# A layer norm and an RMS norm whose factors go through a DRAM row: one change to a hybrid encoder kernel

## The chip, the cores and the metric

The kernel runs on one NeuronCore of a Trainium2 chip. The metric is device time in microseconds (us) for one execution. Engines are named as the profile names them: PE multiplies matrices (PEld loads its weights), DVE is the vector engine, ACT the scalar engine, POOL the GpSimd engine, SP the engine that issues most DMAs. POOL can issue DMAs of its own; it writes their pieces in software.

## The reference, cut to what matters

The reference is one layer of an encoder on an input of 1024 positions by 1024 channels, in float32. Two of its norms are touched:

```
def _rmsnorm(x, w):
    y = x * rsqrt(mean(x * x, axis=-1) + EPS)
    return y * w

def _layernorm(x, w, b):
    mu = mean(x, axis=-1)
    var = mean(square(x - mu), axis=-1)
    return (x - mu) * rsqrt(var + EPS) * w + b

a = silu(_layernorm(_dwconv_centred(glu(...)), ln_w, ln_b))     # 512 channels
...
x  = x + y @ w_out
h2 = _rmsnorm(x, ffn_norm_w)                                    # 1024 channels
x  = x + (silu(dwconv3(h2 @ W_gate)) * (h2 @ W_up)) @ W_down
```

The kernel keeps channels on the 128 partitions and positions along the free axis, so both norms sum over partitions, and the factor of each position has to be spread to all 128 partitions again.

## The kernel before, in words

Every big product is made with float32 values split in two parts of a rounded type (`split`: ACT copies the high part, DVE subtracts it to get the low part), three matmuls of 128x128 weights by 128x512 columns for each pair (`mm3`, lines 148 to 150). Most products run as `pair_job`s: two column blocks of weights are multiplied with one set of activations by seven products instead of eight, in the order 1, 2, 6, 7, 5, 4, 3. Each product is 12 matmuls here. Products 1, 6, 5 and 3 share one PSUM bank (`mm`), 7 and 4 share another (`sc`), 2 has its own (`tr`). When a bank takes its next product, the earlier contents must have been copied out: by ACT at line 440 (tile `su`) for products 1, 6 and 7, so product 6 cannot start before the copy of product 1 is done, product 5 not before the copy of product 6, product 4 not before the copy of product 7.

The norms are slotted between the pieces of such streams. `s_pairs.fill(n)` lets the stream of in-projection pairs advance by n pieces of six matmuls; the statements of the norm stand between two fills. PE keeps exactly the order in which the program states its work; on the other engines a scheduler places instructions when it is built, and then each engine runs its list strictly in order. So an instruction that waits holds back all that stand behind it on its engine.

The layer norm (loop at line 1056, one pass for each half of the positions): the channel sum of the four tiles (`total`) is multiplied by a matrix of ones in plain float32 (line 1065), which gives the mean on all partitions; DVE subtracts it (L1067); ACT squares (L1071); four small matmuls against a column of ones (L611) leave the variance of position 128c+p in column c of a 128x4 tile `r`; DVE copies it out (L615), POOL multiplies and raises to the power -0.5 (L592, L593). To spread it, `spread` makes four diagonal matrices (ACT, L600), multiplies them by ones in plain float32 (L601) and copies the result from PSUM (ACT, L602). Then DVE scales the four tiles (L1077, L1078), ACT applies silu (L1079) and the result is split (tile `ch`) and stored.

The FFN norm does the same for both halves, called `early`: there POOL makes the diagonals (L621). The scaling is late: `evac` of the first FFN job multiplies by `rstd2` (L1682, L1683), and the low parts of the activations of products 4 and 3 of that job (tile `hy`) are made by DVE at the same time. The names `hy`, `wq` and `wp` are the split activations and the split weights of that stream.

`x2_evac`, which ends each out-projection, stores the gained result `g` of all 16 tiles into the DRAM scratch `d_h2`. Later code reads back four of them: those of the second half of positions with index 4 to 7.

Of the kernel before, what the change touches and what calls it, by code (L numbers as in the profile page):

```python
# [18 lines left out]
P = 128  # L19
# [28 lines left out]
def tile_hybrid_encoder(  # L48
# [51 lines left out]
    def bank(tag):  # L100
        return ps.tile([P, H], F32, tag=tag, name=nm(tag), bufs=BANKS[tag])
# [4 lines left out]
    def tmp():  # L106
        return page(mp, "tm", 4)
# [375 lines left out]
    G.memset(mhalf, -0.5)  # L483
    ones_m = cp.tile([P, P], F32, name="ones_m")
    cp.tile([P, ALIGN // 4 - 8], F32, name="offset")
# [83 lines left out]
    d_x2 = scratch("d_x2", ND, 2)  # L569
    d_h2 = scratch("d_h2", ND, 2)  # L570
    d_t4 = scratch("d_t4", ND // 2)
# [22 lines left out]

    def spread(r, b, rs, diag=None, late=False):

        if diag is None:
            diag = tmp()
            for c in range(4):
                A.activation(diag[:, c * P : (c + 1) * P], ident, AF.Copy, scale=r[:, c : c + 1])  # L600
        T.matmul(b, ones_m, diag, start=True, stop=True)  # L601
        do = A.copy(rs, b)  # L602
        if late:
            pin(do)
        return rs

    def rstd_over_partitions(sq, n, tag, rs, early=False):
# [8 lines left out]
        rstd_small(r, r, n, early)  # L616
        diag = None
        if early:
            diag = tmp()
# [436 lines left out]
    for half in range(2):  # L1056
# [7 lines left out]
        mean = bank("ob")  # L1064
        T.matmul(mean, ones_m, total(xs, tmp()), start=True, stop=True)
        for t in xs:
# [6 lines left out]
        next(rstd)  # L1073
        s_pairs.fill(5)
        rs = next(rstd)
# [505 lines left out]
    def x2_evac(i):  # L1581


        def evac(half, acc):
# [178 lines left out]
    for k in range(NK2):  # L1763
        late_parts(5 + k // 2, 3, fetch(d_h2[k + NK2][1]))
    s_ffn.fill(7)
# [303 lines left out]
```

## Time and profile before

| quantity | value |
|---|---|
| median of three runs | 1721.42 us (1721.3 to 1722.16) |
| span of the profiled execution, first to last instruction | 1720.0 us |
| between the span and the median of the runs | 1.4 us |
| PE busy | 1699.1 us, 99% of the span |
| DVE busy | 1256.6 us, 73% |
| ACT busy | 825.0 us, 48% |
| POOL busy | 240.7 us, 14% |
| mean granted PE clock | 0.998 |

The layer norm runs at 406 to 476 us of the span, the out-projection at about 970 to 1055 us and the FFN norm at 1059 to 1078 us. In the rows of the timeline the columns are: start in us, length in us, engine, line, operation, output and input tiles, shapes, how many instructions are merged, and in brackets the idle time ahead with what ended it. Matmul rows overlap, since matmuls are pipelined: the distance between two starts is the time that one costs.

### The profile page before, as it was taken

The numbers are of one execution on the slowest core, as the hardware profiler recorded it, in microseconds if no ns is written. First come the engines' busy times: TensorE is split into PE (matmuls) and PEld (weight loads), VectorE is DVE, ScalarE is ACT, GpSimd is POOL, SyncE is SP. The second block draws the span as 40 slices with busy tenths as digits, with TensorE's granted clock in tenths as the row PEclk, the third lists the DMA queues.
The fourth block names the chain that finished last, engine by engine and source line by source line (L and its number), as shares of the span: only waits on it lengthen the run. The fifth ranks groups of instructions, "written<-read, shape, count | busy, mean of one in ns | idle before, by whom it ended". The sixth has DMA issues, their size and how long they took to land.

```text
span 1720.0 us, 30762 instructions
## 1 busy us (share of the span) xinstructions
PE 1699.1 (99%) x11902; PEld 1416.2 (82%) x11902; DVE 1256.6 (73%) x1937; ACT 825.0 (48%) x1544; POOL 240.7 (14%) x281
## 2 busy tenths in 40 slices
PE   8999999999999999999999999999999999999998
PEld 6878888788788888888888888888888888888787
DVE  4599999745779888888656466667777776657865
ACT  6443443233577777776442245444434433542334
POOL 1212222200001111111100002122222222000110
PEclk9999999999999999999999999999999999999999
DMA  8777888854673444435689466577778776783842
GB/s 281 238 181 177 201 191 189 203 160 148 202 261 91 146 127 133 128 116 200 223 277 279 143 205 199 147 159 153 165 166 174 171 172 154 229 266 102 215 95 99
DMA packets 337096, 308.28 MB, mean 179 GB/s; under 512 B 17582, under 2 KB 249142, under 8 KB 336950
## 3 DMA queue, kind: packets, MB, share of 16 engines
q1 hardware_dynamic: 289590, 267.51, 49.1%
q0 software_dynamic: 47360, 38.81, 15.5%
q8 instruction: 93, 1.52, 0.4%
q14 instruction: 53, 0.43, 0.1%
HBM read 201.40 MB, written 87.03 MB: 168 GB/s over the span
## 4 chain that ended last, share of the span: by engine, by line
PE 61%; DVE 1%; ACT 1%; DMA 0%; issue 0%; POOLq 0%; ACTq 0%; SPq 0%; DVEq 0%
PE mm L148 14%; PE mm L150 14%; PE mm L149 14%; PE sc L148 3%; PE sc L150 3%; PE sc L149 3%; PE ob L1375 2%; PE tr L148 1%; PE tr L150 1%; PE tr L149 1%; PE sc L1197 1%; PE sc L1283 1%; PE mm L1334 1%; PE sc L1334 1%; PE ob L1197 0%
## 5 line engine op out<-in xcount | busy, mean ns | idle before, releaser
L148 PE MATMUL mm<-hx,wp 128*128 128x512 f32 x1068 | 426.9, 400 | 2.3 <-ACT tm L851 1.4
L150 PE MATMUL mm<-hx,wp 128*128 128x512 f32 x1068 | 416.9, 390 | 0.5 <-DVE wp L124 0.5
L149 PE MATMUL mm<-hx,wp 128*128 128x512 f32 x1068 | 416.2, 390 | 0.0
L124 ACT CAST wp<-wr 128x1024 fp32r<-128x1024 f32 (+2 forms) x147 | 147.3, 1003 | 217.8 <-PE mm L149 180.3
L148 PEld LDWEIGHTS mm<-hx,wp 128*128 128x128 f32 x1068 | 200.6, 188 | 45.0 <-DVE ev L800 2.2
L150 PEld LDWEIGHTS mm<-hx,wp 128*128 128x128 f32 x1068 | 200.5, 188 | 44.4 <-DVE wp L124 1.6
L149 PEld LDWEIGHTS mm<-hx,wp 128*128 128x128 f32 x1068 | 200.8, 188 | 39.2 <-issue 0.7
L124 DVE TENSOR_TENSOR wp<-wr,wp 128x1024 fp32r<-128x1024 f32 (+2 forms) x145 | 169.1, 1167 | 39.1 <-ACT wp L124 32.7
L1039 DVE SCALAR_TENSOR_TENSOR acc<-gl,v_b,acc 128x1024 f32<-128x1024 f32 x120 | 148.7, 1272 | 0.4
L440 ACT COPY su<-mm 128x512 f32<-128x512 f32 x82 | 47.7, 582 | 80.1 <-PE mm L150 80.1
L1315 POOL DMA_DIRECT2D S<-D x64 | 36.3, 573 | 284.2 <-ACT S L1313 155.6
L1144 DVE TENSOR_TENSOR qF<-qF,tb 128x512 f32<-128x512 f32 x96 | 65.5, 684 | 13.3 <-ACT A L1178 12.7
L124 ACT CAST wq<-sw 128x1024 fp32r<-128x1024 f32 x41 | 43.2, 1053 | 61.2 <-PE mm L149 32.9
L148 PE MATMUL tr<-hx,wp 128*128 128x512 f32 x180 | 70.5, 392 | 0.0
L150 PE MATMUL tr<-hx,wp 128*128 128x512 f32 x180 | 70.1, 389 | 0.0
L149 PE MATMUL tr<-hx,wp 128*128 128x512 f32 x180 | 70.0, 389 | 0.0
L1144 DVE TENSOR_TENSOR kG<-kG,tb 128x512 f32<-128x512 f32 x96 | 65.5, 685 | 4.7 <-ACT A L1178 2.5
L1652 DVE SCALAR_TENSOR_TENSOR tm<-gp,v_a,tm 128x512 f32<-128x512 f32 x88 | 66.0, 750 | 4.0 <-ACT tm L1650 2.0
L301 POOL DMA_DIRECT2D sw<-in_ffn_w_up_dram x38 | 49.8, 1498 | 116.5 <-DMA sw<-in_ffn_w_up_dram 76.7
L148 PE MATMUL mm<-hy,wp 128*128 128x512 f32 x164 | 64.2, 391 | 0.0
L148 PE MATMUL sc<-hy,wq 128*128 128x512 f32 x164 | 64.2, 391 | 0.0
L150 PE MATMUL sc<-hy,wq 128*128 128x512 f32 x164 | 63.8, 389 | 0.0
(375 smaller groups left out, 3723.3 us busy)
## 6 DMA issues: line engine op xcount, KB each, us to landing
wr<-in_w_in_dram SPq DMA_DIRECT2D x48, 512.0 KB, 5.0
wr<-in_ffn_w_up_dram SPq DMA_DIRECT2D x22, 512.0 KB, 5.1
sw<-in_w_in_dram SPq DMA_DIRECT2D x38, 256.0 KB
d_g<-ft SPq DMA_DIRECT2D x38, 256.0 KB, 2.0
sw<-in_ffn_w_up_dram SPq DMA_DIRECT2D x38, 256.0 KB, 3.5
sw<-in_ffn_w_up_dram POOLq DMA_DIRECT2D x38, 256.0 KB, 6.2
wr<-sw POOLq DMA_DIRECT2D x32, 256.0 KB, 3.3
wr<-wr POOLq DMA_DIRECT2D x32, 256.0 KB, 3.4
```

The costliest lines, as they stand in the source:

```text
L124: parts = A.copy(hi, src), eng.tensor_tensor(lo, src, hi.bitcast(F32), op=ALU.subtract)
L148: T.matmul(acc, whi[:, k, :], ahi, start=first, stop=False, skip_group_check=again)
L149: T.matmul(acc, whi[:, k, :], alo, start=False, stop=False, skip_group_check=again)
L150: T.matmul(acc, wlo[:, k, :], ahi, start=False, stop=last, skip_group_check=again)
L301: G.dma_start(o, a, accum_op=ALU.add)
L440: A.copy(t, acc)
L1039: V.scalar_tensor_tensor(acc, g[:, k : k + S], tap(k), acc, op0=ALU.mult, op1=ALU.add)
L1144: return V.tensor_tensor(o, a, b, op=op)
L1315: G.dma_start(S_t[g : g + 32, :, g : g + 32], D_t[g : g + 32])
L1334: T.matmul(u[:, sl], kTs[d][:, sl], v[:, c, :], start=True, stop=True)
L1375: T.matmul(o[:, sl], l, r, start=(n == 0), stop=(n == len(terms) - 1))
L1652: V.scalar_tensor_tensor(c, g[:, o + k : o + k + H], vec("fdw", k * NF + j), c, op0=ALU.mult, op1=ALU.add,)
```

## The change: what it does

Three edits.

1. **The spread.** `rstd_over_partitions` no longer makes diagonals and no longer calls `spread`. POOL writes the 128x4 tile `r` into a DRAM row of 512 floats (`row`, transposed by its access pattern) and then loads that row to all 128 partitions by an access pattern with step 0. Both DMAs stand on POOL's queue behind the power, and the load waits for the write to land. This holds for both passes of the layer norm and for both halves of the FFN norm. Only the input norm still uses `spread`.
2. **The mean.** The channel sum is split in high and low part, and two matmuls against ones of the rounded type replace the plain float32 matmul. The layer norm now lets 7 pieces run instead of 5 between the variance and the scaling.
3. **The stores.** `d_h2` keeps only the four tiles that are read.

```
-    ones_m = cp.tile([P, P], F32, name="ones_m")
+    ones_r = cp.tile([P, P], F32R, name="ones_m")
+    ones_m = ones_r.bitcast(F32)
...
         rstd_small(r, r, n, early)
-        diag = None
-        if early:
-            diag = tmp()
-            pin(
-                G.tensor_tensor(
-                    diag.rearrange("p (c e) -> p c e", c=4),
-                    view(ident, 0, [[0, 4], [1, P]]),
-                    view(r, 0, [[1, 4], [0, P]]),
-                    op=ALU.mult,
-                )
-            )
+        row = dp.tile([4, P], F32, name=nm("d_row"))
+        G.dma_start(row.rearrange("c p -> p c"), r)
+        G.dma_start(rs, bass.AP(tensor=row.tensor, offset=row.offset, ap=[[0, P], [1, H]]))
         yield
-        yield spread(r, bank(tag), rs, diag, early)
+        yield rs
...
         mean = bank("ob")
-        T.matmul(mean, ones_m, total(xs, tmp()), start=True, stop=True)
+        sums = split(*(page(mp, "tm", 4, F32R) for _ in range(2)), total(xs, tmp()), V)
+        for n, part in enumerate(sums):
+            T.matmul(mean, ones_r, part, start=n == 0, stop=n == 1)
...
         next(rstd)
-        s_pairs.fill(5)
+        s_pairs.fill(7)
         rs = next(rstd)
...
             A.activation(g, t, AF.Copy, scale=vec("ffn", i))
-            nc.sync.dma_start(d_h2[i][half], g)
+            if i >= NK2 and half:
+                nc.sync.dma_start(d_h2[i], g)
```

The scheduler answers with another order at three places. Line numbers of the changed program are some 8 to 10 lower: its L1069, L1070 and L1071 are L1077, L1078 and L1079 of before.

ACT in the first pass of the layer norm, before (from the copy of the spread, L602, to the copy of product 6, `su_3939`) and then in the change (the same stretch; `su_3875` is the copy of product 1 and `su_3931` that of product 6):

```order
L805 COPY ev_3865<-mm_3665 128x512
L602 COPY tm_3779<-ob_3825 128x512
L440 COPY su_3883<-mm_3868 128x512
L1079 ACTIVATE cx_3635<-cx_3635 128x512 x2
L124 CAST ch_3836<-cx_3635 128x512
L124 CAST ch_3844<-cx_3635 128x512
L124 CAST wp_3905<-wr_3897 128x1024
L1079 ACTIVATE cx_3638<-cx_3638 128x512
L124 CAST ch_3852<-cx_3638 128x512
L1079 ACTIVATE cx_3638<-cx_3638 128x512
L124 CAST ch_3860<-cx_3638 128x512
L440 COPY su_3939<-mm_3868 128x512
```

```order
L795 COPY ev_3825<-mm_3657 128x512
L1071 ACTIVATE cx_3627<-cx_3627 128x512 x2
L124 CAST ch_3846<-cx_3627 128x512
L124 CAST ch_3854<-cx_3627 128x512
L440 COPY su_3875<-mm_3828 128x512
L1071 ACTIVATE cx_3630<-cx_3630 128x512 x2
L124 CAST ch_3862<-cx_3630 128x512
L124 CAST ch_3870<-cx_3630 128x512
L124 CAST wp_3897<-wr_3889 128x1024
L440 COPY su_3931<-mm_3828 128x512
```

The copy of product 1 has moved behind the first two silus and their splits.

DVE in the second pass, around the copy of the variance out of PSUM (L615 before, L613 in the change; `ev_4151` in both is the evacuation of product 4):

```order
L800 TENSOR_TENSOR ev_4136<-su_4101,mm_4006 128x512
L615 COPY r_646_4132<-ob_4127 128x4
L124 TENSOR_TENSOR wq_4062<-sw_4047,wq_4061 128x1024
L800 TENSOR_TENSOR ev_4151<-sc_4008,su_4087 128x512
L124 TENSOR_TENSOR wq_4069<-w_631_4059,wq_4069 128x512
```

```order
L790 TENSOR_TENSOR ev_4112<-su_4098,mm_3998 128x512
L124 TENSOR_TENSOR wq_4044<-sw_4029,wq_4043 128x1024
L790 TENSOR_TENSOR ev_4151<-sc_4000,su_4084 128x512
L124 TENSOR_TENSOR wq_4051<-w_630_4041,wq_4051 128x512
L613 COPY r_650_4144<-ob_4139 128x4
```

The copy has moved three rows back, behind the evacuation of product 4; its matmuls (L609 in the change) stand 12 matmuls later on PE too.

DVE at the FFN norm: the rows around the first use of the factor (L1682 before, L1675 with `gp` in the change, where L1668 is the L1675 of before):

```order
L124 TENSOR_TENSOR hy_12251<-ft_12165,hy_12250 128x512
L124 TENSOR_TENSOR hy_12255<-tm_12112,hy_12254 128x512
L124 TENSOR_TENSOR wq_12266<-w_2002_12173,wq_12266 128x512
L124 TENSOR_TENSOR wp_12270<-wr_12205,wp_12269 128x1024
L124 TENSOR_TENSOR hy_12290<-ft_12221,hy_12289 128x512
L1675 TENSOR_TENSOR ft_12311<-su_12281,mm_12148 128x512
L124 TENSOR_TENSOR hy_12294<-ft_12223,hy_12293 128x512
L124 TENSOR_TENSOR hy_12304<-ft_12225,hy_12303 128x512
L124 TENSOR_TENSOR hy_12308<-ft_12227,hy_12307 128x512
L1682 TENSOR_TENSOR gp_12142<-gp_12142,rs_11395 128x512
```

```order
L124 TENSOR_TENSOR hy_12233<-ft_12145,hy_12232 128x512
L1675 TENSOR_TENSOR gp_12122<-gp_12122,rs_11387 128x512
L124 TENSOR_TENSOR hy_12237<-tm_12092,hy_12236 128x512
L124 TENSOR_TENSOR wq_12248<-w_2004_12153,wq_12248 128x512
L124 TENSOR_TENSOR wp_12252<-wr_12187,wp_12251 128x1024
L124 TENSOR_TENSOR hy_12272<-ft_12203,hy_12271 128x512
L1668 TENSOR_TENSOR ft_12293<-su_12263,mm_12128 128x512
L124 TENSOR_TENSOR hy_12276<-ft_12205,hy_12275 128x512
L124 TENSOR_TENSOR hy_12286<-ft_12207,hy_12285 128x512
L124 TENSOR_TENSOR hy_12290<-ft_12209,hy_12289 128x512
```

The use of the factor has moved ahead of eight rows: it now stands before the low parts (`hy_12237`, `wq_12248`) that product 4 of the first FFN job needs.

More of the change, by code (lines that the diff above doesn't have):

```diff
@@ L569, in tile_hybrid_encoder @@
     d_x2 = scratch("d_x2", ND, 2)
-    d_h2 = scratch("d_h2", ND, 2)
+    d_h2 = scratch("d_h2", ND)
     d_t4 = scratch("d_t4", ND // 2)
@@ L593, in rstd_small, with spread @@
         hold(G.tensor_tensor(dst, dst, mhalf.to_broadcast(list(dst.shape)), op=ALU.pow))
-    def spread(r, b, rs, diag=None, late=False):
-        if diag is None:
-            diag = tmp()
-            for c in range(4):
-                A.activation(diag[:, c * P : (c + 1) * P], ident, AF.Copy, scale=r[:, c : c + 1])
+    def spread(r, b, rs):
+        diag = tmp()
+        for c in range(4):
+            A.activation(diag[:, c * P : (c + 1) * P], ident, AF.Copy, scale=r[:, c : c + 1])
         T.matmul(b, ones_m, diag, start=True, stop=True)
-        do = A.copy(rs, b)
-        if late:
-            pin(do)
+        A.copy(rs, b)
         return rs
@@ L1763, in tile_hybrid_encoder @@
     for k in range(NK2):
-        late_parts(5 + k // 2, 3, fetch(d_h2[k + NK2][1]))
+        late_parts(5 + k // 2, 3, fetch(d_h2[k + NK2]))
     s_ffn.fill(7)
```

1 line of the change is left out of this document (removed).

## The prediction

> **What bounds the kernel now.** I read the page's header and engine shares first, then the windows by stage, then the timelines of the three places that the change touches, then the DMA issues. The header and shares, and two windows (columns: window, length, busy time of PE, PEld, DVE, ACT, POOL, clock, DMA share, GB/s):
>
> ```profile
> span 1720.0 us, 30762 instructions
> PE 1699.1 (99%) x11902; PEld 1416.2 (82%) x11902; DVE 1256.6 (73%) x1937; ACT 825.0 (48%) x1544; POOL 240.7 (14%) x281
> ...
> 960.00:1000.00 40.00, 40.00 (x178) 33.10 (x178) 20.18 (x29) 14.15 (x21) 0.00 (x0) 1.00 0.55 170
> 1000.00:1056.00 56.00, 56.00 (x249) 46.37 (x248) 31.55 (x45) 24.60 (x37) 0.00 (x0) 1.00 0.60 194
> ```
>
> PE has work at every moment but 1720.0 - 1699.1 = 20.9 us. So a matmul taken off PE's list is worth its slot, and a wait that PE newly meets costs its full length: nothing is there to absorb it.
>
> What a plain float32 spread costs on PE is the gap in the ordinary rhythm (PE timeline, first pass of the layer norm):
>
> ```profile
> 422.51 0.40 PE L150 MATMUL mm<-hx,wp 128*128 128x512 f32 x1
> 422.74 1.02 PE L601 MATMUL ob<-tm,ones_m 128*128 128x512 f32 x2
> ...
> 424.07 0.39 PE L150 MATMUL mm<-hx,wp 128*128 128x512 f32 x1
> 424.30 0.39 PE L148 MATMUL mm<-hx,wp 128*128 128x512 f32 x1
> ```
>
> One split matmul costs 424.30 - 424.07 = 0.23. Three of them and the float32 one lie between 422.51 and 424.07: 1.56 - 0.69 = 0.87 for the spread. The mean's matmul has the same shape and type, so 0.87 too; its two replacements cost 0.46.
>
> **The change, part by part.** *Stores.* Twelve stores of 256 KB go, all issued between the two windows above, where PE is busy 40.00 of 40.00 and 56.00 of 56.00 us. There is no gap to win: 0. Were the DMA engines (0.55 to 0.60 busy) short, PE would show waits there.
>
> *Mean.* 2 x (0.87 - 0.46) = 0.82 less on PE. The sum's last addition and the mean's matmul in the second pass, where they are closest:
>
> ```profile
> 444.79 0.69 DVE L1053 TENSOR_TENSOR tm<-tm,cx 128x512 f32<-128x512 f32 x1
> 449.19 1.02 PE L1065 MATMUL ob<-tm,ones_m 128*128 128x512 f32 x2
> ```
>
> The added split (an ACT copy and a DVE subtraction per pass, 0.6 to 0.7 each) fits into the 3.7 us between them; uncovered it would cost 1.3.
>
> *Spread.* Four spreads leave PE: 4 x 0.87 = 3.48. With the mean 4.3 us, 0.25%, is all that PE can win on its own slots. Against it stands a new chain that begins when POOL's power ends: issue of the write, landing, issue of the load, landing. I call its length L. The nearest rows (issue times on POOL by form: min/median/max ns; then landings from the list of DMA issues, last column median us; the last row is that of the S<-D copies):
>
> ```profile
> L301 POOL DMA_DIRECT2D sw<-in_ffn_w_up_dram x38: 1288/1303/1892, 1097.8 to 1441.5; - x38
> L301 POOL DMA_DIRECT2D wr<-sw x32: 862/887/897, 125.7 to 1450.2; - x32
> L1315 POOL DMA_DIRECT2D S<-D x64: 549/552/792, 524.0 to 848.2; - x64
> ...
> sw<-in_ffn_w_up_dram POOLq DMA_DIRECT2D x38, 256.0 KB, 6.2
> cx<-d_cv SPq DMA_DIRECT2D x8, 256.0 KB, 2.7
> d_x<-x SPq DMA_DIRECT2D x16, 256.0 KB, 2.0
> S<-D POOLq DMA_DIRECT2D x64, 16.0 KB, 2.7
> DMA to landing us min/median/max: 1.6/2.7/5.2
> ```
>
> The write has 128 x 4 pieces of 4 bytes, as many pieces as the sw row (128 x 4 of 512 bytes): issue 1.3. Its landing is unknown in this trace: at least the quickest S<-D, 1.6, at most that of the accumulating POOL transfer in 512 pieces, 6.2; I take the median of POOL's only plain copy, 2.7. The load has 128 pieces of 2 KB: issue between 0.55 (S<-D, 128 pieces) and 0.89 (wr<-sw, accumulating), so 0.7; landing between 2.0 (d_x) and the 5.2 at the top of S<-D, and I take that of cx<-d_cv, a plain load of the same size and shape, 2.7. L = 1.3 + 2.7 + 0.7 + 2.7 = 7.4. The low end is 0.55 + 1.6 + 0.55 + 2.0 = 4.7, the high end 1.3 + 6.2 + 0.89 + 5.2 = 13.6.
>
> The page "DMA: Bandwidth & Descriptors" of the Trainium skill (section "Anatomy of one DMA — SWDGE (gpsimd) path") gives a fixed cost of about 2.0 us for each DMA plus its bytes over 436 GB/s; by that the write would land in 2.0 and the load in 2.6, and the whole sum below would be near +0.5 us. Its section "Rules for kernel authors" says that a non-contiguous last dimension becomes one descriptor per element; that speaks against this write, and no run here has shown such a DMA yet.
>
> *First pass.* The rows (DVE, ACT, PE and POOL timelines):
>
> ```profile
> 416.58 1.03 POOL L593 TENSOR_TENSOR r<-r,mhalf 128x4 f32<-128x4 f32 x1
> 427.62 1.28 DVE L1077 TENSOR_TENSOR cx<-cx,tm 128x512 f32<-128x512 f32 x2
> 428.83 1.00 DVE L1078 TENSOR_SCALAR cx<-cx,v_a 128x512 f32<-128x512 f32 x2
> 429.74 1.28 DVE L1077 TENSOR_TENSOR cx<-cx,tm 128x512 f32<-128x512 f32 x2
> 431.40 1.28 DVE L124 TENSOR_TENSOR ch<-cx,ch 128x512 fp32r<-128x512 f32 x2
> 433.06 1.22 DVE L124 TENSOR_TENSOR wp<-wr,wp 128x1024 fp32r<-128x1024 f32 x1
> 429.41 1.15 ACT L1079 ACTIVATE cx<-cx 128x512 f32<-128x512 f32 x2 [2.28 <-DVE cx L1078]
> 430.47 1.13 ACT L124 CAST ch<-cx 128x512 fp32r<-128x512 f32 x2
> 431.50 1.04 ACT L124 CAST wp<-wr 128x1024 fp32r<-128x1024 f32 x1
> 435.45 0.50 PE L148 MATMUL mm<-hy,wq 128*128 128x512 f32 x1 [0.79 <-ACT su L440]
> ```
>
> Here product 5 already waits 0.79 for ACT's copy of product 6. In the new ACT list that copy still stands behind all four silus. Counting from the landed factor: DVE two scalings 1.2, two affine 0.9, one weight split 1.15, two scalings 1.2, two low parts 1.2 and the first affine 0.55 make 6.2; ACT then needs two silus and two splits, 2.3, the weight copy 0.95 and the copy itself 0.55: 10.0. The power ends at 417.6, 0.4 earlier by the cheaper mean: 417.2. So product 5 starts at 417.2 + L + 10.05 = 427.25 + L, against 435.45 before: **L - 8.2**, at best -(0.41 + 0.87 + 0.79) = -2.07, where PE alone sets it. At 7.4: -0.8. (Product 6 then already waits for the copy of product 1, which stands 4.55 behind the factor; it is the same delay, not another.)
>
> *Second pass.* The rows:
>
> ```profile
> 460.69 1.01 POOL L593 TENSOR_TENSOR r<-r,mhalf 128x4 f32<-128x4 f32 x1
> 462.10 0.69 DVE L800 TENSOR_TENSOR ev<-sc,su 128x512 f32<-128x512 f32 x1 [1.55 <-PE sc L150]
> 463.55 0.69 DVE L124 TENSOR_TENSOR wq<-w,wq 128x512 fp32r<-128x512 f32 x1 [0.76 <-ACT wq L124]
> 479.11 0.39 PE L148 MATMUL sc<-hx,wq 128*128 128x512 f32 x1
> ```
>
> The copy of the variance now follows the evacuation of product 4, which comes 1.25 earlier (0.41 of the mean, and the small matmuls no longer ahead of it): 460.85, then 0.6 and 0.6 for it and the weights' low part, 0.2 for the copy, and POOL's two steps, 1.3 with their hand-overs. The power ends at 463.8 instead of 461.7. ACT's copy of product 7, for which product 4 of the last pair waits, stands behind four silus as before; from the factor DVE takes 5.7 to the third affine (scalings, affine and low parts as above, one evacuation between them), ACT 1.15 + 1.05 + 0.55: 8.45. Product 4 starts at 463.8 + L + 8.5 against 479.11: **L - 6.8**, at best -1.28. At 7.4: +0.6. The two more pieces of fill do not help, since by the order of the lists it is the same copies that wait.
>
> *FFN norm.* The rows:
>
> ```profile
> 1065.13 1.33 POOL L593 TENSOR_TENSOR r<-r,mhalf 128x4 f32<-128x4 f32 x1
> 1066.81 1.32 DVE L124 TENSOR_TENSOR hy<-ft,hy 128x512 fp32r<-128x512 f32 x1 [0.62 <-ACT hy L124]
> 1068.05 0.68 DVE L124 TENSOR_TENSOR hy<-tm,hy 128x512 fp32r<-128x512 f32 x1
> 1068.65 0.68 DVE L124 TENSOR_TENSOR wq<-w,wq 128x512 fp32r<-128x512 f32 x1
> 1071.37 0.39 PE L150 MATMUL sc<-hy,wq 128*128 128x512 f32 x1
> 1072.05 0.40 PE L150 MATMUL sc<-hy,wq 128*128 128x512 f32 x1
> ...
> 1074.46 0.40 PE L150 MATMUL sc<-hy,wq 128*128 128x512 f32 x1
> ```
>
> In the new order DVE meets the use of the first factor right after the `hy` row that ends at 1068.1, and holds there until the load has landed, 1066.46 + L. Behind it stand `hy`, then `wq`, whose low part the third matmul of product 4 needs: 0.05 + 0.6 + 0.6 + 0.68 + 0.1 = 2.05 later. That matmul stood at 1071.37. With the two spreads gone PE wins 1074.46 - 1072.05 - 0.69 = 1.72. Net: 1066.46 + L + 2.05 - 1071.37 - 1.72 = **L - 4.6**, at best -1.72. At 7.4: +2.8. What follows (weights, `hy` of product 3, at 0.6 to 1.15 each) keeps up with PE. The second factor waits on POOL behind the first load; its two POOL steps and its own L end it near 1066.5 + 4.7 + 1.8 + 7.4 = 1080.4, and product 3 ends 22 matmuls after the stall, near 1081: no further stall.
>
> *Sum* at L = 7.4: -0.8 + 0.6 + 2.8 = **+2.6 us**, on a span of 1720.0. That span stands 1.4 under the median of the runs, so 1721.4 + 2.6 = **1724.0 us**. The three places share L: 3L - 19.6. The gain of 4.3 is eaten.
>
> **The rivals.** *Short hop*: the write lands like the quickest plain store, 2.0, so L = 6.7: -1.5 - 0.1 + 2.1 = +0.5, 1721.9. For it: DMAs are few at these moments of the layer norm. Against: 512 tiny pieces. By the skill's rule above, the same.
>
> *Gain collected*: L at its low end, 4.7, gives -2.07 - 1.28 + 0.1 = -3.3, 1718.1. For it: 1.6 has been seen for a copy of 128 pieces. Against: all four parts would have to be at their minimum, and even then DVE waits at the FFN norm, since 1066.46 + 4.7 is past 1068.1. Only a gain not counted here would go beyond.
>
> *Slow write*: slower. 512 pieces of 4 bytes land halfway between S<-D and the accumulating transfer in 512 pieces, (2.7 + 6.2)/2 = 4.4, so L = 9.1: +0.9 + 2.3 + 4.5 = +7.7, 1729.1. Its place is POOL's wait between the two DMAs. For it: as many pieces as the 6.2 row. Against: that one accumulates and carries 256 KB. It decides from L = 7.7 on, where the sum passes 3.4 us.
>
> *The change does not do what it says*: the write and load do replace the matmuls, and the order shows it; only the stores could be a rival, with nothing (1724.0 stays).
>
> **How the numbers follow.** 0.2% (3.4 us) is about what a measurement of this kernel tells from no change. Forecast case 0.42, of which 0.30 stay within 0.2% and 0.12 pass it, since the threshold is only 0.3 in L away; short hop 0.18, within; gain collected 0.14, of which 0.08 faster; slow write 0.26. So faster 0.08, same 0.54, slower 0.38. Range 1719.0 (L = 5.5) to 1729.5 (L = 9.2, the slow write's price): the tails are the lower half of the gain case and the upper part of the slow one. The likeliest case alone spans L of 6.9 to 8.0: 1722.5 to 1725.8.
>
> **What would show it.** On POOL, write and load: their issue times, and the wait between them, give L. DVE at the FFN norm should idle some 6 us before the first `gp` times `rs`, ended by a DMA, and PE some 4.5 us in product 4 right behind. In the layer norm PE should wait for ACT's `su` copies, 1.3 us in all in the first pass and 1.9 in the second. PE's busy time should fall. It is wrong if DVE's idle time there is under 3 us, if PE waits for other things, or if the out-projection's windows change.

## The result: slower, and the profile after

| quantity | before | after |
|---|---|---|
| median of the runs (4 each) | 1721.55 us | 1763.24 us (1762.61 to 1766.6) |
| ratio, 95% interval | | 1.0244 [1.0233, 1.0256] |
| span of the profiled execution | 1720.0 us | 1760.8 us |
| mean granted PE clock | 0.998 | 0.987 |

The change makes the kernel 41.7 us slower. The forecast was 1724.0 us in a range of 1719.0 to 1729.5, so it was wrong, and by much; slower, the direction that came, had a chance of 0.38.

The header and the shares of the page of after:

```profile
span 1760.8 us, 30718 instructions
PE 1703.4 (97%) x11894; PEld 1419.1 (81%) x11894; DVE 1257.3 (71%) x1939; ACT 822.2 (47%) x1534; POOL 241.7 (14%) x287
```

PE has less work than before, yet its busy time rose by 4.3 us, and its idle time from 20.9 to 57.4 us. Its matmuls took longer behind the stalls, as shown below. Where it waits is told by the view of PE's waits (waiting instruction and what it waited for; us in total, times, longest):

```profile
PE mm L148 <- ACT su L440: 21.5, 2, 11.0
PE sc L150 <- DVE wq L124: 12.1, 1, 12.1
```

These are the three places that the prediction named: two copies `su` in the layer norm, and the third matmul of product 4 (`wq`) behind the FFN norm. The size is another matter. The view of each line's DMAs, the write first, then the load (ns min/median/max of the issue, first and last start; then the landing):

```profile
L616 POOL DMA_DIRECT2D d_row<-r x4: 819/824/843, 418.1 to 1104.6; - x4
DMA to landing us min/median/max: 9.5/9.8/10.4
```

```profile
L617 POOL DMA_DIRECT2D tm<-d_row x2: 560/574/587, 428.5 to 486.2; - x2
...
DMA to landing us min/median/max: 3.9/6.5/7.1
```

2 KB need 9.8 us to land. The landing counts from the start of the issue: the load issued at 1102.39 (rows below) has a landing of 3.9, and DVE uses its data at 1106.35. How that reaches PE in the layer norm, from the timelines of POOL, DVE and PE (the rows of the first pass, and power and first use of the second):

```profile
416.81 1.04 POOL L594 TENSOR_TENSOR r<-r,mhalf 128x4 f32<-128x4 f32 x1
418.15 0.84 POOL L616 DMA_DIRECT2D d_row<-r  x1 [0.30 <-POOL r L594]
428.47 0.59 POOL L617 DMA_DIRECT2D tm<-d_row  x1 [9.48 <-DMA d_row<-r]
434.64 1.29 DVE L1069 TENSOR_TENSOR cx<-cx,tm 128x512 f32<-128x512 f32 x2 [12.80 <-DMA tm<-d_row]
439.14 0.79 PE L148 MATMUL mm<-hy,wp 128*128 128x512 f32 x1 [10.56 <-ACT su L440]
439.73 0.63 PE L149 MATMUL mm<-hy,wp 128*128 128x512 f32 x1
440.15 0.63 PE L150 MATMUL mm<-hy,wp 128*128 128x512 f32 x1
...
447.44 0.39 PE L148 MATMUL mm<-hy,wq 128*128 128x512 f32 x1
474.41 1.04 POOL L594 TENSOR_TENSOR r<-r,mhalf 128x4 f32<-128x4 f32 x1
493.32 1.29 DVE L1069 TENSOR_TENSOR cx<-cx,tm 128x512 f32<-128x512 f32 x2 [14.88 <-DMA tm<-d_row]
```

From the power's end, 417.85, to DVE's first use, 434.64, pass 16.8 us: that is L here, made of 0.3 to the issue, 9.8 for the write, 0.5 to the next issue and 6.2 for the load. In the second pass it is 493.32 - 475.45 = 17.9. Behind the stall the matmuls stand 440.15 - 439.73 = 0.42 apart, where 0.23 is the rhythm: PE runs at half its clock (the granted clock is 0.50 from 439.1 to 444.2 us). The FFN norm, from the same timelines:

```profile
1089.82 1.33 POOL L594 TENSOR_TENSOR r<-r,mhalf 128x4 f32<-128x4 f32 x1
1091.44 0.83 POOL L616 DMA_DIRECT2D d_row<-r  x1 [0.29 <-POOL r L594]
1102.39 0.57 POOL L617 DMA_DIRECT2D rs<-d_row  x1 [10.12 <-DMA ft<-d_h]
1104.64 0.82 POOL L616 DMA_DIRECT2D d_row<-r  x1 [0.29 <-POOL r L594]
1114.68 0.57 POOL L617 DMA_DIRECT2D rs<-d_row  x1 [9.22 <-issue]
1106.35 0.69 DVE L1675 TENSOR_TENSOR gp<-gp,rs 128x512 f32<-128x512 f32 x1 [14.14 <-DMA rs<-d_row]
1121.57 0.69 DVE L1676 TENSOR_TENSOR gp<-mm,rs 128x512 f32<-128x512 f32 x1 [6.77 <-DMA rs<-d_row]
1123.44 0.50 PE L150 MATMUL mm<-hx,wp 128*128 128x512 f32 x1 [1.31 <-DVE wp L124]
```

L is 1106.35 - 1091.15 = 15.2. The second hop begins only when POOL is through with the first, so the second factor comes another 15.2 us later, and PE, though it ran slowly for a while, still meets it and waits 1.31.

To see how much each stage costs, I compare when the same ACT instruction starts in both kernels; how much later it starts is called the lag. Rows of ACT's timeline, before:

```profile
328.23 0.59 ACT L440 COPY su<-mm 128x512 f32<-128x512 f32 x1 [1.41 <-PE mm L150]
413.87 0.59 ACT L440 COPY su<-sc 128x512 f32<-128x512 f32 x1 [2.19 <-PE sc L150]
449.15 1.05 ACT L124 CAST wp<-wr 128x1024 fp32r<-128x1024 f32 x1 [1.90 <-PE tr L149]
518.69 0.62 ACT L1178 COPY A<-kG 128x512 f32<-128x512 f32 x1
1060.84 0.58 ACT L440 COPY su<-mm 128x512 f32<-128x512 f32 x1
1157.20 0.59 ACT L440 COPY su<-mm 128x512 f32<-128x512 f32 x1 [1.85 <-PE mm L150]
```

The same six, after:

```profile
327.24 0.59 ACT L440 COPY su<-mm 128x512 f32<-128x512 f32 x1 [1.41 <-PE mm L150]
414.11 0.59 ACT L440 COPY su<-sc 128x512 f32<-128x512 f32 x1 [2.19 <-PE sc L150]
461.06 1.06 ACT L124 CAST wp<-wr 128x1024 fp32r<-128x1024 f32 x1 [1.95 <-PE tr L149]
542.81 0.62 ACT L1170 COPY A<-kG 128x512 f32<-128x512 f32 x1
1085.54 0.58 ACT L440 COPY su<-mm 128x512 f32<-128x512 f32 x1
1196.80 0.59 ACT L440 COPY su<-mm 128x512 f32<-128x512 f32 x1 [1.85 <-PE mm L150]
```

The lag goes from -0.99 over +0.24, +11.91, +24.12 and +24.70 to +39.60. So the first pass costs 11.7 us, the second 12.2, the FFN norm 14.9, together 38.8; 1.2 are lost on the way to the layer norm, before any row is written; the out-projection, where the stores went, gives and takes nothing (the lag is 24.7 at 968 us of the kernel before and still 24.7 at 1055).

### The profile page after: what moved, and what is told of

Read it like the earlier page. It is cut to its first block, busy times and chain, and to the rows that moved or that the text cites. A ratio compares the mean times of both kernels' runs of the same rounds, so it can differ in the third digit from the quotient of the medians.

```text
span 1760.8 us, 30718 instructions
## 1 busy us (share of the span) xinstructions
PE 1703.4 (97%) x11894; PEld 1419.1 (81%) x11894; DVE 1257.3 (71%) x1939; ACT 822.2 (47%) x1534; POOL 241.7 (14%) x287
## 4 chain that ended last, share of the span: by engine, by line
PE 58%; DMA 2%; DVE 2%; issue 1%; ACT 1%; SPq 0%; POOLq 0%; ACTq 0%; DVEq 0%
PE mm L148 13%; PE mm L150 13%; PE mm L149 13%; PE sc L150 3%; PE sc L148 3%; PE sc L149 3%; PE ob L1367 2%; PE tr L148 1%; PE tr L150 1%; PE tr L149 1%; PE sc L1189 1%; DMA rs<-d_row 1%; DMA ft<-d_h 1%; PE sc L1275 1%; PE mm L1326 1%
## 5 line engine op out<-in xcount | busy, mean ns | idle before, releaser
L150 PE MATMUL sc<-hy,wq 128*128 128x512 f32 x164 | 64.9, 396 | 12.1 <-DVE wq L124 12.1
L148 PE MATMUL mm<-hy,wp 128*128 128x512 f32 x164 | 65.2, 397 | 10.6 <-ACT su L440 10.6
L149 PE MATMUL mm<-hy,wp 128*128 128x512 f32 x164 | 65.0, 396 | 0.0
```

The costliest lines, as they stand in the source:

```text
L148: T.matmul(acc, whi[:, k, :], ahi, start=first, stop=False, skip_group_check=again)
L149: T.matmul(acc, whi[:, k, :], alo, start=False, stop=False, skip_group_check=again)
L150: T.matmul(acc, wlo[:, k, :], ahi, start=False, stop=last, skip_group_check=again)
```

## The experiments

All ratios are against the kernel before, run on the same chip beside them, with 95% intervals. The code shown is cut to what matters.

**1 to 3: the change cut into its parts.** The theory was that the row alone makes the loss, in three places that add up; the rival that the mean or the stores have a share. The first kernel keeps the old spread, and takes over the split mean and the dropped stores:

```diff
-        row = dp.tile([4, P], F32, name=nm("d_row"))
-        G.dma_start(row.rearrange("c p -> p c"), r)
-        G.dma_start(rs, bass.AP(..., ap=[[0, P], [1, H]]))
+        (diagonals and spread as before)
-        s_pairs.fill(7)
+        s_pairs.fill(5)
```

> The change without its DRAM row: split mean and dropped stores stay, the spread by diagonals and the fill of 5 come back. Theory (everything lost was lost at the row): 0.8 us under the kernel before, about 1720.7, two matmul slots of 0.87 replaced by 0.46 each, and nothing from the stores. Rival (the dropped stores or the split sums upset the order elsewhere): clearly over 1722.

Measured: 1723.85 us, 1.0008 [0.9999, 1.0017], where a gain was expected. The gain of the cheaper mean is not there. ACT's, DVE's and PE's timelines of this kernel show why:

```profile
340.14 0.62 ACT L124 CAST tm<-tm 128x512 fp32r<-128x512 f32 x1 [4.69 <-DVE tm L1054]
340.79 0.69 DVE L124 TENSOR_TENSOR tm<-tm,tm 128x512 fp32r<-128x512 f32 x1 [0.74 <-ACT tm L124]
341.40 0.68 DVE L801 TENSOR_TENSOR ev<-su,mm 128x512 f32<-128x512 f32 x1
342.14 0.50 PE L148 MATMUL mm<-hx,wp 128*128 128x512 f32 x1 [1.92 <-DVE ev L801]
```

The same `ev` in DVE's timeline of before:

```profile
341.15 0.68 DVE L800 TENSOR_TENSOR ev<-su,mm 128x512 f32<-128x512 f32 x1
```

In the first pass ACT and DVE reach the mean's sum some 65 us ahead of PE, and the sum waits there for the loads of `cx` (the mean's own matmul starts at 405.94 before). The split's new copy on ACT (`tm<-tm`) waits for the sum, DVE's new subtraction waits for the copy, and `ev` stands behind the subtraction in DVE's queue. So it starts at 341.40 against 341.15 before, although this kernel was 1.6 us ahead by then, and PE waits 1.9 for it in place of 0.7. From 343.2 to 346.7 us the granted clock is 0.51. At this one place the lag rises by 3.5 us, from -1.6 to +1.9.

> The row only in the layer norm; the FFN norm spreads by diagonals again. Theory: each place pays for itself. In the changed kernel PE waited 10.6 and 11.0 us in the two passes and ran slower for a while behind each wait; less the slots won and the old wait of 0.8, and with about 4 us of slow clock each, 12.5 + 13.7 = 26 us: about 1747.6. Rival (the places share a cause, as bulk transfers moved by one stall into the next): a sum that does not add up with the run that has the row only in the FFN norm.

This one has the row in the layer norm alone (`if not early:` around it, the FFN norm with diagonals). Measured: 1748.61 us, 1.0154 [1.0141, 1.0168].

> The row only in the FFN norm; the layer norm spreads by diagonals again, with the split mean. Theory: 12.1 us of wait, less 1.7, plus about 4 us of slow clock, less the mean's 0.8: 13.6 us, about 1735.1. Rival as before: no sum with the run that has the row only in the layer norm.

And this one has the row in the FFN norm alone. Measured: 1738.27 us, 1.0095 [1.0081, 1.0109]. The two are 26.4 and 16.1 us over before, 42.5 together; each holds the 1.6 that run 1 measured for the rest of the change (its interval reaches from 0 to 2.9), which counts once, so 40.9 are expected of both and 41.7 are there. The three places add up, and the row makes the loss.

**4: the write in pieces of 16 bytes.** The row keeps the order of the tile `r`, so each partition writes its four values side by side; the scalings undo the order with a view of the factors.

```diff
-        row = dp.tile([4, P], F32, name=nm("d_row"))
-        G.dma_start(row.rearrange("c p -> p c"), r)
+        row = dp.tile([P, 4], F32, name=nm("d_row"))
+        G.dma_start(row, r)
...
-            V.tensor_tensor(xn, xn, rs, op=ALU.mult)
+            V.tensor_tensor(by_c(xn), by_c(xn), by_q(rs), op=ALU.mult)
```

> The row is written in the tile's own order, 128 pieces of 16 bytes instead of 512 of 4, and read back as a permuted row, which the users undo by their access patterns; every list of instructions stays as in the changed kernel. Theory (the write's landing of 9.5 to 10.4 us goes with the number of its pieces): landing near 4 us, every chain some 6 us shorter, about 1739 us or less. Rival (a write into DRAM that a load waits for takes this long however it is cut, or it queues behind bulk transfers): landing stays over 8 us, 1763.

Measured: 1739.39 us, 1.0097 [1.0083, 1.0111]. The write in this kernel's view by line:

```profile
L622 POOL DMA_DIRECT2D d_row<-r x4: 611/622/630, 417.9 to 1082.5; - x4
...
DMA to landing us min/median/max: 1.7/1.8/5.1
```

The landing is 8 us less in the median, where I expected 6. L at the three places is 10.2, 8.3 and 9.4 here, 22 us less in all, and the time falls by 24: about 1 us for 1 us, as the prediction had it. The landing of the write is the largest cause. That it is the number of pieces does not follow, since their size changed too; runs 10, 14 and 15 take that up.

**5: a PE that is kept busy in the stalls.** All DVE, ACT and POOL work stays; matmuls of ones go to a bank that nobody reads.

```diff
+    # ahead of the stalled matmul of the second pass (46) and of the FFN norm (50):
+    T.matmul(spare_bank, ones_r, view(ones_r, 0, [[0, 4], [1, P]]), start=True, stop=True)
```

> The changed kernel with matmuls that nobody reads laid into two of its three stalls: 46 of them (all ones, into the spare bank) ahead of the matmul that waits 10.96 us in the second pass, and 50 ahead of the one that waits 12.07 us in the FFN norm; the lists of VectorE, ScalarE and GpSimd are unchanged. At 0.227 us each they fill 10.4 and 11.4 us, a little less than the stalls, so the stalls' ends stay where they are. Theory (an idle TensorE loses its clock and is paid for a second time): in the changed kernel about 13 matmuls behind each stall stand 0.427 us apart instead of 0.227, 2.6 us a stall; with TensorE kept busy they stand 0.227 apart, and the time falls by about 5, from 1763.2 to 1758. Rival (the waits alone make the loss; the slow matmuls are a habit of the records, or come from something other than the idling): 1763, and the matmuls behind the stalls still 0.427 apart.

Measured: 1766.2 us, 1.0257 [1.0241, 1.0273]: the time did not fall. PE's timeline of this kernel (rows of equal matmuls are merged, the count is at the end):

```profile
487.64 10.62 PE L153 MATMUL ob<-ones_m 128*128 128x512 f32 x46
498.09 2.92 PE L154 MATMUL mm<-hy,wq 128*128 128x512 f32 x12
...
1124.01 4.11 PE L154 MATMUL mm<-hx,wp 128*128 128x512 f32 x10 [3.81 <-DVE wp L124]
```

The clock did what the theory says: behind the second pass' stall 12 matmuls take 2.92 us, at full rhythm. Against the changed kernel the lag of ACT's rows falls by 1.5 us there (from +0.65 to about -0.9), less than the 2.6 expected. At the FFN norm the gain is taken by another wait: PE runs faster, reaches the matmuls that hang on the second factor sooner, and waits 3.81 where it waited 1.31; that wait in turn costs the clock again (10 matmuls in 4.1 us). There the lag grows by 1.5. Another 2 us were lost far from the edit, between 821 and 862 us; why was not looked into. So the theory that a busy PE alone recovers the loss fell.

**6 and 11: is it the single row?** The load reads the same 2 KB 128 times. Two kernels on the base of run 4 read 128 different rows instead.

```diff
-        G.dma_start(rs, bass.AP(tensor=row.tensor, offset=row.offset, ap=[[0, P], [1, H]]))
+        G.dma_start(rs, row)          # row: 128 rows of 2 KB, the first one written
```

> The kernel with the 16-byte write, whose load now reads 128 different rows of a DRAM tile of 256 KB instead of one row 128 times; only the first row holds the deviations, the others hold data of the convolution, so the scaled values are wrong. Four stores of 256 KB during the convolution fill the tile and are hidden. Theory A (128 reads of the same 2 KB of DRAM make the load slow, 6.5 us in the layer norm against 2.7 for the plain load of cx): the landing falls to about 3 in the layer norm, VectorE's wait there from 11.5 in two times to about 5, and the time from 1739.4 to about 1732. Theory B (the load is slow since it shares the DMA engines with other transfers at that moment): landing and time stay, 1739 +-1.5.

Measured: 1739.46 us, 1.0094 [1.008, 1.0108], as theory B has it, but the experiment was spoiled: against run 4 the lag rises by 4.1 us between 300 and 383 us, where the four added stores go, and falls by 2.4 in the layer norm. So it was made again without added stores:

> The kernel with the 16-byte write, whose load reads 128 different rows, this time of the convolution's own tile in DRAM, which has been read by then, so that no store is added (in the run before this one four added stores cost 4 us in the convolution, and hid what the load did); the factors are wrong but for the first row. Every engine's list is that of the kernel with the 16-byte write. Theory A (reading one row 128 times makes the load slow): the load lands in 3 to 5 us instead of 5.6 to 7.4 in the layer norm, and the time falls by 2 to 5, from 1739.4 to 1734.5 to 1737.5. Theory B (other transfers on the same DMA engines make it slow): landing and time stay, 1739 +-1.

Measured: 1735.17 us, 1.0074 [1.006, 1.0088]. The loads' landing in run 4, and then in this one:

```profile
DMA to landing us min/median/max: 3.4/4.9/7.4
```

```profile
DMA to landing us min/median/max: 2.9/3.5/6.2
```

Load for load, in the order of time, 7.4, 5.6, 3.4 and 4.1 us have become 6.2, 4.1, 2.9 and 2.9: reading one row costs 0.5 to 1.5 us a load, in favour of theory A, though only one of the two loads of the layer norm came into its 3 to 5 us. Of the 3.5 us between the two spans 1.0 stand ahead of the layer norm already and are chance; 1.5 fall in the second pass and 0.7 at the FFN norm. Most of the load's excess over 2.7 stays even so, and the runs do not tell why: with the one row read 128 times, run 10 has 3.6 and 4.0 us from issue to first use in the two passes, run 4 has 7.5 and 5.7. The traces point to other transfers: of the 16 loads of one row in the change and in runs 4, 10 and 14, the five during which the DMA engines were busy less than 0.35 of the time landed in 3.4 to 3.9 us, the eleven at 0.50 or more in 4.0 to 7.4. No run changed the other transfers alone, so that they are the cause is not shown.

**7: the mean's split without ACT.**

```diff
-        sums = split(hi, lo, total(xs, tmp()), V)     # ACT copies the high half
+        V.tensor_copy(hi, t)
+        V.tensor_tensor(lo, t, hi.bitcast(F32), op=ALU.subtract)
```

> The kernel with the old spread, the mean by split sums and the stores dropped, whose rounded high half of the sum is now copied by VectorE and not by ScalarE. Theory (the split cost 1.9 us of wait in the first pass, and a slow clock behind it, since ScalarE's copy of the high half, which waits for the sum, stands in ScalarE's queue ahead of the weights' copies): without it the queue is free, TensorE's wait at that place goes back to 0.8 or less, the 0.8 us of the cheaper mean appears, and the time is 1721.4 against 1722.2 before, ratio 0.9995, against 1.0008 with ScalarE's copy. Rival (the split sums cost something else, or the dropped stores do): 1723.9, as with ScalarE's copy.

Measured: 1722.33 us, 1.0000 [0.9991, 1.0008] against 1.0008 before it. The interval holds the theory's 0.9995 and, at its edge, the rival's 1.0008, so I go by the trace. PE's wait for `ev` falls from 1.9 to 1.1, and the clock stays at 1.00 behind it. But DVE's own copy and subtraction (0.43 and 0.69 us) now stand ahead of `ev` in DVE's queue, and the lag against before still rises by 1.0 at this place, from -1.8 to -0.8. Through the layer norm it falls by 0.7, close to the 0.8 of the cheaper mean. So the cheaper mean does win its slots here, and the split ahead of `ev` takes them back; ACT's queue was only a part of it.

**8 and 12: can the hop be hidden?** The scalings are pinned behind 12 pieces of fill instead of 7, the write has 16-byte pieces, the FFN norm the old spread.

```diff
-            V.tensor_tensor(xn, xn, rs, op=ALU.mult)
+            pin(V.tensor_tensor(by_c(xn), by_c(xn), by_q(rs), op=ALU.mult))
-        s_pairs.fill(7)
+        s_pairs.fill(12)
-LN_LAST = 12
+LN_LAST = 7
```

> The row in the layer norm alone, written in 16-byte pieces, with the scalings kept behind 12 pieces of fill (before 7; 7 instead of 12 follow them), the high half of the mean's sum copied by VectorE, the FFN norm with the old spread, the stores dropped. ScalarE's copies of the products now stand ahead of the silus. Theory (what the row costs is only what stands behind it in the two queues, so a hop with other work ahead of it costs nothing, and TensorE keeps the slots of two spreads, 1.7, of the mean, 0.8, and of the old wait of 0.8): 1719 to 1720.5, ratio 0.998 to 0.999. Rival (the wait only goes to the next use of the late values, or the hop of 9 us is still longer than the work put ahead of it): above 1723, with TensorE's waits for ScalarE's copies still there.

Measured: 1739.68 us, 1.0096 [1.0082, 1.011]: the rival, and by more than it said. PE's waits in this kernel:

```profile
PE sc L1217 <- ACT A L1198: 6.0, 4, 4.3
PE ob L1085 <- DVE tm L1082: 5.1, 1, 5.1
```

The waits for `su` are gone, and the first pass is 1.7 us quicker by the lag. But the late scalings hold the buffers of `cx`, so the second pass' mean waits 5.1 us for its sum, and behind the second pass there is no fill left: the next stage's copies (`A`) stand behind the late silus. Behind both of these waits the granted clock is 0.50 as well (454.8 to 461.6 and 516.2 to 523.1 us); the two waits and the clock together make up the rise of the lag from the second pass on, some 15.5 us. Run 12 therefore keeps the row to the first pass, gives the second pass' mean five more pieces of fill, and has the old spread elsewhere.

> The row in the first pass of the layer norm alone, written in 16-byte pieces, its scalings kept behind 12 pieces of fill; the mean of the second pass stands behind 11 pieces of fill instead of 6, and fewer follow each pass, so that the sum is that of before; the second pass and the FFN norm have the old spread; the mean's split on VectorE, the stores dropped. Theory (a hop hides where enough other work stands between it and its use: the first pass then gains the slot of a spread and the old wait of 0.8, 1.7 in all, as the first pass of the last such kernel did, and with the mean 0.4 to 0.8): 1719.8 to 1720.8 against 1722.0 before, ratio 0.9988 to 0.9993. Rival (the late scalings hold the convolution's buffers, and the second pass starts late as in the last such kernel, where the mean waited 5.1 us): 1724 or more.

Measured: 1723.34 us, 1.0004 [0.9995, 1.0013]. By the lag it gains 1.1 us between 399 and 527 us, and no stall is left; the timing cannot tell it from before, and neither the theory nor the rival is met. None of the kernels tried beats the kernel before.

**9 and 13: the two hops of the FFN norm.** Both writes are issued before the first load; then PE is kept busy as well.

```diff
+            pin(write)
+            yield
         G.dma_start(rs, bass...)
...
-    for st in stats:
+    for st in stats + stats:
         next(st)
```

> The changed kernel whose FFN norm issues both writes of a row before the first load; on GpSimd the first load moves behind the second power and the second write, and nothing else moves. Theory (the two hops of the FFN norm stand in series on GpSimd, which waits 9.2 to 10.1 us between write and load, so the second factor comes 15.2 us behind the first and its wait, not only the first, sets the end: in the changed kernel the FFN norm costs 14.9 us, of which the first hop explains 15.2 - 4.6 = 10.6): with the landings overlapped VectorE's second wait of 6.8 us falls below 2, and the FFN norm costs 11 to 13, so the time falls by 2 to 4, from 1763.2 to 1760. Rival (512 pieces of 4 bytes keep the DMA engines themselves busy, so that two writes at once take twice as long): both factors come at about the time at which the second comes now, VectorE's first wait grows from 14.1 to over 20, and the time is 1763 or more.

Measured: 1759.29 us, 1.0215 [1.0201, 1.0229]. The total is as expected, but by luck: only 1.05 of the 4 us were won at the FFN norm (the lag against the changed kernel goes from -2.54 to -3.59); 1.4 came in the layer norm (from -0.6 to -2.0), whose second hop was 0.5 shorter by chance, and the rest is spread over the run. DVE's second wait is gone. What stands there instead, in the timelines of DVE and PE:

```profile
1104.85 0.69 DVE L1678 TENSOR_TENSOR gp<-gp,rs 128x512 f32<-128x512 f32 x1 [15.18 <-DMA rs<-d_row]
1106.80 0.79 PE L150 MATMUL sc<-hy,wq 128*128 128x512 f32 x1 [13.10 <-DVE wq L124]
...
1107.81 0.63 PE L149 MATMUL sc<-hy,wq 128*128 128x512 f32 x1
1108.24 0.63 PE L150 MATMUL sc<-hy,wq 128*128 128x512 f32 x1
```

The first hop grew by 1.0: its write landed in 11.6 us, with the second write under way at the same time. That this is the reason is not shown, for in run 13, with the same two writes, it landed in 10.2. The slow matmuls, 0.43 apart, now set the end; run 13 tries that.

> The kernel with both writes of the FFN norm ahead of the loads, and 54 matmuls that nobody reads (all ones, 0.227 us each, 12.3 us) ahead of the matmul that waits 13.1 us there; no other list changes. Theory (in the changed kernel two things ended the FFN norm at nearly the same time, the second factor and the slow matmuls behind the stall, so taking away either alone gave 0 to 1 us; with both gone the first hop alone is left): the FFN norm falls by 2 to 2.6 us more, and the time from 1759.3 to 1757, with the matmuls behind the stall 0.227 us apart. Rival (the slow matmuls never cost time here, since VectorE and ScalarE are behind by as much): 1759.

Measured: 1756.83 us, 1.0203 [1.0186, 1.022]. The ten matmuls behind the stall:

```profile
1106.21 2.56 PE L153 MATMUL sc<-hy,wq 128*128 128x512 f32 x10
```

Against run 9 the lag falls by 2.78 us at this place, of which 0.7 is a shorter first hop and 2.1 the clock. The FFN norm now costs 14.9 - 1.05 - 2.78 = 11.1 us; its L is 15.5 (1088.72 to 1104.26), so the prediction's formula gives 10.9. With the second hop and the slow clock gone, the first hop alone is left, and the formula holds. These figures are lags of one trace each; the timings of runs 9 and 13 differ by 2.5 us, with intervals that just overlap.

**10, 14 and 15: why does the write take 9.8 us?** Number, size of the pieces, or queue. The power writes each value four times (run 10) or twice (run 14), so that 512 pieces have 16 or 8 bytes:

```diff
+        wide = cp.tile([P, 4, 4], F32, ...)       # run 14: [P, 4, 2]
-        row = dp.tile([4, P], F32, name=nm("d_row"))
-        G.dma_start(row.rearrange("c p -> p c"), r)
+        row = dp.tile([4, P, 4], F32, name=nm("d_row"))
+        G.dma_start(row.rearrange("c p e -> p c e"), wide)
```

> The changed kernel whose write has again 512 pieces, but of 16 bytes instead of 4: the power writes each deviation four times side by side, and the row in DRAM is four times as long. The load reads its first 2 KB, so its size and pieces are as before, but the factors are the wrong ones and the output is wrong. Theory (the number of pieces makes the landing of the write: 9.5 to 10.4 us for 512, 1.7 to 1.8, once 5.1, for 128): the landing stays at 9 to 10.5 and the time at 1763 +-2. Rival (a piece of 4 bytes is what is slow): the landing falls to between 1.7 and 4, and the time to about 1742, near the kernel with 128 pieces of 16 bytes.

> As the kernel with 512 pieces of 16 bytes, with pieces of 8 bytes (each deviation written twice; the factors are wrong). Theory (a piece of DRAM that is written costs the more the smaller it is below 16 bytes): the landing lies between 3.9 and 9.8 us, some 6, and the time near 1750. Rival (only 4-byte pieces are slow): landing 2.3 to 5.9 as with 16 bytes, time some 1740, less 1 to 2 us since the power of 8 columns is shorter than that of 16.

> The changed kernel whose write of 512 pieces of 4 bytes is issued by SyncE's queue instead of GpSimd's (the load stays on GpSimd); the lists of the other engines move a little with it, so the landing is what is read and not the time. Theory (the pieces of 4 bytes are slow in the DMA engines or in DRAM): it lands in 9 to 10.5 us again. Rival (GpSimd's queue is slow with such pieces): it lands in under 5.

The last one only changes `G.dma_start` of the write to SyncE's. The landings, in this order (run 10, 14, 15; in run 15 the view has a landing for one of the four writes only):

```profile
DMA to landing us min/median/max: 2.3/3.9/5.9
```

```profile
DMA to landing us min/median/max: 3.3/4.6/6.0
```

```profile
DMA to landing us min/median/max: 9.3/9.3/9.3
```

Times: 1741.44 us, 1.0116 [1.01, 1.0131], for 16 bytes; 1745.16, 1.0133 [1.0112, 1.0153], for 8; 1762.78 in one run for the other queue. In run 15 the load is issued 9.7 to 11.5 us behind the write at all four places, against 10.0 to 11.0 in the changed kernel. My theory that the number of pieces makes the landing fell: 512 pieces of 16 bytes land in 3.9 us, of 8 bytes in 4.6, of 4 bytes in 9.8; 128 of 16 bytes in 1.8. Four times the pieces, with four times the bytes, cost some 2 us, and the step from 8 to 4 bytes 5 us; for 8 bytes the landing is nearer to the rival's, and the time lies between the two. GpSimd's queue is not the cause, since SyncE's is as slow. One rival is left: smaller pieces also lie closer together in DRAM, and no run wrote pieces of 4 bytes 16 bytes apart, so size and spacing are not told apart.

The page "DMA: Bandwidth & Descriptors" of the Trainium skill (section "Specifications") says that transfers under 512 bytes are done by reading, changing and writing back. Pieces of 16 bytes lie under that as well as those of 4, so this alone does not tell 1.8 from 9.8. The fit that the prediction took from the same page of the Trainium skill (section "Anatomy of one DMA — SWDGE (gpsimd) path"), 2.0 us plus the bytes over 436 GB/s, knows no size of pieces. By the fit the write would land in 2.0 us, an estimate, and 1.8 agrees with it for 128 pieces of 16 bytes; for 512 of 4 bytes 9.8 was measured, and the measurement decides.

## Why the prediction was wrong, step by step

- **What bounds.** Right as far as it went: PE was the bound, and every wait that it newly met showed in the time. But "a wait that PE newly meets costs its full length" was too little. Behind waits of 11 to 13 us PE ran at half its clock for some 5 us. The sum had no term for it. It was worth 1.5 us in the second pass (run 5) and 2.1 at the FFN norm (run 13 against 9). By the page "TensorE: Matmul & The Clock Gate" of the Trainium skill (section "What's actually happening") the clock halves after about 3.4 us of idling; the granted clock of 0.50 behind these stalls agrees, but run 1 shows it behind a wait of 1.9 us too, where matmuls stand 0.43 apart from 343.5 us on, and run 4 shows 1.00 behind one of 2.2 us.
- **Stores: 0.** Right: no gain and no loss in the out-projection.
- **Mean: -0.82, hidden.** Wrong, by the place where its cover was looked up. The cover of 3.7 us is the second pass'; in the first pass DVE and ACT are far ahead of PE, the sum waits for its loads, and the new copy and subtraction stand in their queues ahead of the `ev` that PE needs. In the changed kernel the lag rises by 1.6 us at 342 us, where PE waits 1.7 for `ev`, and falls by 0.4 at the mean itself: the 1.2 of the lags above.
- **Length of the hop, L.** This is the step that failed, and it carries the error: 7.4 was taken, 16.8, 17.9 and 15.2 were measured, above even the high end of 13.6. The issues were cheaper than priced (0.82 for 1.3, 0.57 for 0.7), and they should not have been added at all, since the landing of the profile holds the issue already. With two landings of 2.7 and 0.8 for the steps between, L would have been 6.2, further still from the truth: this error went the lucky way. "Its landing is unknown ... at most that of the accumulating POOL transfer in 512 pieces, 6.2; I take the median of POOL's only plain copy, 2.7": measured 9.8. The bound came from a row with as many pieces, but of 512 bytes, and the 2.7 from pieces of 128 bytes (16 KB in 128); runs 10 and 14 show that pieces of 4 bytes cost far more than those of 8 or 16. The landing of the load was taken as 2.7 and bounded by 5.2: measured 6.5 in the median, and why is open (runs 6 and 11).
- **The three places and their order.** Right: `su`, `su` and `wq`, with DVE waiting for the load at each; in the two passes PE met the wait one product earlier than the one that the formula is written for. The formulas with the measured L give 16.8 - 8.2 = 8.6, 17.9 - 6.8 = 11.1 and 15.2 - 4.6 = 10.6, in all 30.3 of the 38.8 us that the three places cost. What they lack is 3.1, 1.1 and 4.3. The 1.1 are no more than the 1.5 of clock that run 5 measured; the 4.3 are the second hop and the clock, which end together (runs 9 and 13). The 3.1 of the first pass are mostly clock: product 6 starts 4.5 behind the factor, as counted (4.55), and from there PE never waits, but the 24 matmuls up to product 5 take 447.44 - 439.14 = 8.3 us where the rhythm of 0.23 makes 5.5. That is read from the trace; no run took the slow matmuls away there alone.
- **FFN norm: "no further stall".** Wrong. At L = 7.4 the second factor would have come in time; at 15.2 the two hops in series on POOL made DVE wait another 6.8 us. So beyond L of 7.4 this place has two terms in L, not one.
- **Rivals.** The slow write had the right mechanism and place, "POOL's wait between the two DMAs", and stood at 0.26; its price, 4.4 for the landing, was halfway between two rows that both lay far under the truth. The range ended with it, although the prediction's own high end for L, 13.6, gives +21 by its sum. The fit of the page "DMA: Bandwidth & Descriptors" of the Trainium skill, put into the formulas, makes by estimate L = 6.6 and +0.2, not the +0.5 that the prediction names.

## What to carry to other kernels

A DMA that writes single float32 values across partitions took five times as long to land as the same 2 KB in 16-byte pieces (9.8 for 1.8 us); even with those, the kernel stayed 1% behind the one before. Where such a hop is needed, lay out the DRAM row so that each partition writes what it holds in one piece, and let the reader's view undo the order. Before work is put into an engine's queue, look at every pass in which it runs, and at what stands behind it, not at the pass where it is closest to its use. Where two waits end at about the same time, taking away one shows nothing, so take away both before a cause is ruled out.

## What the runs showed of the hardware that was not expected

- Landing of a 2 KB write from 128 partitions: 1.8 us as 128 pieces of 16 bytes, 9.8 as 512 of 4 bytes from POOL's queue and 9.3 from SP's; 512 pieces of 8 and 16 bytes, which carry twice and four times the bytes, 4.6 and 3.9.
- PE ran at half its clock behind a wait of 1.9 us (run 1) as well as behind those of 11, and at its full clock behind waits of 1.7 (the change, at 342 us) and 2.2 (run 4, at 482 us). The stretches with a granted clock of 0.50 last whole multiples of 3.41 us in these traces: 3.41 in run 1, 13.65 at each of the three stalls of the change, which takes in part of the wait ahead.
- POOL's power takes 1.04 us for 4 columns, 1.67 for 8 and 2.93 for 16. DVE's scaling of 128x512 takes 1.07 us instead of 0.69 when the factors are read with a stride of four.
